# A two-layer decoder trunk on one core: in the slabs beside the top-k chain, the lo part of one expert table slab in four is subtracted on GpSimd

## The chip, the cores and the metric

The kernel runs on one core of a Trainium2 chip. A core has TensorE (PE in the profile; its weight loads are PEld), VectorE (DVE), ScalarE (ACT), GpSimd (POOL) and the queue of SyncE (SP), which issues the loads. Each works through its own instructions in order and waits for the others by semaphores. The metric is the device time of one execution in microseconds (us), lower being better. TensorE's granted clock is shown by the profile for every stretch.

## The reference

A trunk of two residual layers works on 256 tokens of width 1024. Layer 0 mixes the tokens with a gated delta rule and block-sparse attention, layer 1 with latent attention. Behind each mixer stands the same expert network (PEER), and only this one is touched by the change:

```
scores = einsum('bshpd,hpnd->bshpn', q, sub_keys)        # 8 heads, 2 halves, 128 keys
s1, i1 = top_k(scores[..., 0, :], 16);  s2, i2 = top_k(scores[..., 1, :], 16)
cand   = s1[..., :, None] + s2[..., None, :]             # 256 candidates per head
top, pos = top_k(cand, 16); expert = i1 * 128 + i2 at pos; gates = softmax(top)
act = gelu(h . u[expert]);  out = sum over experts of gates * act * v[expert]
```

There are 16384 experts, so u and v are tables of 16384 x 1024 floats per layer. 8 heads x 16 experts are chosen for each token.

## The kernel before, in words

The kernel doesn't gather the chosen rows. It multiplies all tokens with the whole table u, 128 experts at a time, and later keeps the chosen ones with a matrix of gates. 128 experts x 1024 floats are a slab; a layer has 128 of u and 128 of v.

Products run in a reduced float format (fp32r). To keep precision, a table slab is split into two parts: hi is the slab rounded to fp32r (a copy on ScalarE), and lo is the slab minus hi (a subtraction on VectorE); `split` (L130) issues both. `u_slab` (L610) loads a slab (512 KB, tile `raw`, 3 buffers), splits it (tiles `hi` and `lo`, 2 buffers each), and issues 16 matmuls with hi as the weights (L621) and then 8 with lo (L623). Each has 256 columns, one for each token. `u_pair` (L749) does two slabs and then one gelu on ScalarE (L759).

Beside the first 64 slabs of a layer stands the top-k chain (`choose`, `topk`), which chooses the experts from the scores. It runs on VectorE. For each of the two token tiles it has two parts. The first takes maxima: 16 per row, by the instructions MAX8, MATCH_REPLACE8 and FIND_INDEX8 (L486 to L499), for 8 heads and 2 halves, and then on the candidates. The second, called the selection arithmetic here, turns positions into expert numbers: comparisons, products and sums over bf16 tiles of 128 x 1024 and smaller (L566 to L583, sums at L518 and L521); all its operands lie in SBUF. Three transposes on TensorE (L604) end the work of a tile. The exponentials of the gates (L552) are ScalarE's and need its table exchanged.

The chain is a generator. `u_pair` takes steps from it after each slab until the steps' sizes pass STEP = 800. All of this is traced under `in_order("DVE")`, so VectorE executes it exactly as written: lo of a slab, a portion of the chain, lo of the next slab, a portion, and so on; after some pairs comes a modulation product (L349). On the other engines a planner puts the instructions in order with a cost model. TensorE's order, as the profile shows it, is slab after slab, 16 and 8. SP's queue issues the loads in order, each when its buffer is free, that is when hi and lo of the slab three before have read it.

Behind the 64 slabs with the chain come 64 slabs of u beside the building of the gate matrix (`g_batch`), and then the products with v, whose slabs are split in the same way. These are not touched.

The functions below are those that the change touches and what calls them.

Of the kernel before, what the change touches and what calls it, by code (L numbers as in the profile page):

```python
# [9 lines left out]
F32 = mybir.dt.float32  # L10
# [57 lines left out]
class Trunk:  # L68
# [58 lines left out]
        nc.vector.memset(self.eps, RS * EPS / 4)  # L127


    def split(self, hi, lo, src):  # L130

        return self.nc.scalar.copy(hi, src), self.nc.vector.tensor_sub(lo, src, hi.bitcast(F32))  # L132

    def mm3(self, out, l, r, start, stop):
        mm = self.nc.tensor.matmul
# [471 lines left out]
        nc.vector.tensor_scalar(dst[:, 2, s], ps[:, 2], GS, None, op0=OP.mult)  # L607
        nc.vector.scalar_tensor_tensor(dst[:, 3, s], ps[:, 2], GS, dst[:, 2, s], op0=OP.mult, op1=OP.subtract)

    def u_slab(self, st, layer, i2, hT, pair):  # L610

        nc = self.nc
        raw = self.t(st, [P, D], tag="raw", bufs=3)
        nc.sync.dma_start(raw, self.a["uT"][layer, i2])
        hi = self.t(st, [P, KD, P], F32R, tag="hi", bufs=2)
        lo = self.t(st, [P, KD, P], F32R, tag="lo", bufs=2)
        self.split(hi.rearrange("p k e -> p (k e)"), lo.rearrange("p k e -> p (k e)"), raw)
        mm = nc.tensor.matmul
        for k in range(KD):
            for s in range(2):  # L620
                mm(pair, hi[:, k], hT[:, s, k], start=k == 0 and s == 0, stop=False)  # L621
        for k in range(KD):
            mm(pair, lo[:, k], hT[:, 0, k], start=False, stop=k == KD - 1)  # L623
# [125 lines left out]
    def u_pair(self, st, layer, i2, hT, act, chain=()):  # L749

        ps = self.ps().rearrange("p (j t) -> p j t", j=2)
        for j in range(2):
            self.u_slab(st, layer, i2 + j, hT, ps[:, j])
            left = STEP
            for n in chain:
                left -= n + 64
                if left < 0:
                    break
        self.nc.scalar.activation(self.act_of(act, i2), ps, AF.Gelu)  # L759
# [1121 lines left out]
```

## Time and profile before

| | |
|---|---|
| time before, median of 3 runs | 1913.13 us (1910.81 to 1915.3) |
| profiled execution | 1913.58 us, span 1911.8 us |
| PE busy | 1878.6 us, 98% of the span |
| DVE busy | 1532.3 us, 80% |
| ACT busy | 943.5 us, 49% |
| POOL busy | 48.9 us, 3%, 131 instructions |
| mean granted clock of TensorE | 0.997 of full speed |
| shares of the chain that ended last | PE 82%, DVE 9%, DMA 4%, ACT 3% |

The profile is of one execution. Busy time is the time in which an engine has an instruction running. The chain that ended last is followed back from the last instruction, at each step to what released it. In the rows "x16" is a count of merged instructions, and what stands in brackets is how long the engine was idle before and what ended it. "out<-in" names tiles.

The slabs with the chain run from about 264 to 440 us in layer 0 and from about 1165 to 1342 us in layer 1.

### The profile page before, as it was taken

Reading aid. Unit: us, or ns where it says so; the run is one execution under the profiler, and the core shown is the slowest. Engines: PE = TensorE matmul, PEld = TensorE weight load, DVE = VectorE, ACT = ScalarE, POOL = GpSimd, SP = SyncE. Lnnn points to the kernel's source line nnn. Section 1 sums busy time; section 2 is a strip of 40 time slices with the busy share of each in tenths; the row PEclk is TensorE's granted clock in tenths of the full one; section 3 lists DMA queues with packets and bytes.
Section 4 is the critical chain, followed back from the end, with each engine's and each line's share of the span. In section 5 each row is a group of like instructions: output and inputs, shape, how many; then the busy total and the mean of one; then the engine's idle time right before and its main releaser. Section 6 shows DMA issues by size and latency. Waiting matters only on the chain.

```text
span 1911.8 us, 35995 instructions
## 1 busy us (share of the span) xinstructions
PE 1878.6 (98%) x14368; PEld 1722.2 (90%) x14368; DVE 1532.3 (80%) x3265; ACT 943.5 (49%) x1301; POOL 48.9 (3%) x131
## 2 busy tenths in 40 slices
PE   6999999999999999999999999999999999999998
PEld 6999899999999888888889899999999988888886
DVE  7879789999998789865657677999778878985565
ACT  2866555454444444454545754545444444444453
POOL 7001000000000000000000000000000000000000
PEclk9999999999999999999999999999999999999999
DMA  8456475658885555576743455565555555556673
GB/s 324 160 194 214 191 279 187 201 187 284 295 270 187 177 177 177 176 251 195 216 147 111 155 201 175 183 203 186 180 175 170 176 177 176 176 180 199 194 228 103
DMA packets 96504, 374.57 MB, mean 196 GB/s; under 512 B 11856, under 2 KB 12112, under 8 KB 89680
## 3 DMA queue, kind: packets, MB, share of 16 engines
q1 hardware_dynamic: 96336, 372.28, 58.4%
q8 instruction: 112, 1.84, 0.4%
q14 instruction: 56, 0.46, 0.1%
HBM read 371.18 MB, written 1.05 MB: 195 GB/s over the span
## 4 chain that ended last, share of the span: by engine, by line
PE 82%; DVE 9%; DMA 4%; ACT 3%; issue 1%; SPq 0%; ACTq 0%; DVEq 0%
PE ps L776 30%; PE ps L621 21%; PE ps L623 11%; PE ps L136 3%; PE ps L138 3%; PE ps L137 3%; PE ps L644 3%; DVE lo L132 3%; DMA raw<-in_v_dram 2%; PE ps L729 1%; DVE t L349 1%; PE ps L324 1%; ACT hi L132 1%; PE ps L1200 1%; DVE wlo L132 1%
## 5 line engine op out<-in xcount | busy, mean ns | idle before, releaser
L132 ACT CAST hi<-raw 128x1024 fp32r<-128x1024 f32 x508 | 534.8, 1054 | 753.1 <-PE ps L776 310.5
L132 DVE TENSOR_TENSOR lo<-raw,hi 128x1024 fp32r<-128x1024 f32 x508 | 620.0, 1222 | 249.0 <-ACT hi L132 246.8
L621 PE MATMUL ps<-hT,hi 128*128 128x256 f32 x4096 | 514.2, 278 | 0.0
L621 PEld LDWEIGHTS ps<-hT,hi 128*128 128x128 f32 x4096 | 485.8, 188 | 0.2 <-ACT hi L132 0.2
L623 PE MATMUL ps<-hT,lo 128*128 128x256 f32 x2048 | 276.7, 278 | 2.0 <-DVE lo L132 1.9
L776 PE MATMUL ps<-hi,vwh 128*128 128x512 f32 x976 | 266.1, 394 | 1.2 <-ACT hi L132 1.1
L776 PE MATMUL ps<-hi,vwl 128*128 128x512 f32 x976 | 261.3, 389 | 0.0
L776 PE MATMUL ps<-lo,vwh 128*128 128x512 f32 x976 | 260.9, 389 | 0.0
L623 PEld LDWEIGHTS ps<-hT,lo 128*128 128x128 f32 x2048 | 252.4, 188 | 4.1 <-DVE lo L132 3.7
L776 PEld LDWEIGHTS ps<-hi,vwl 128*128 128x128 f32 x976 | 183.2, 188 | 38.8
L776 PEld LDWEIGHTS ps<-lo,vwh 128*128 128x128 f32 x976 | 183.2, 188 | 38.3
L776 PEld LDWEIGHTS ps<-hi,vwh 128*128 128x128 f32 x976 | 180.3, 188 | 38.1 <-ACT hi L132 2.9
L132 DVE TENSOR_TENSOR wlo<-wraw,whi 128x1024 fp32r<-128x1024 f32 (+1 forms) x84 | 99.3, 1202 | 36.1 <-ACT whi L132 36.0
L132 ACT CAST whi<-wraw 128x1024 fp32r<-128x1024 f32 (+1 forms) x84 | 84.3, 1032 | 36.5 <-PE ps L137 14.2
L640 DVE TENSOR_TENSOR ohG<-ohB,t 128x512 f16<-128x512 f16 x256 | 99.3, 418 | 0.0
L136 PE MATMUL ps<-hT,whi 128*128 128x256 f32 x288 | 85.0, 296 | 7.1 <-ACT hT L247 7.1
L634 DVE TENSOR_TENSOR ohA<-t,t 128x1024 f16<-128x1024 f16 x128 | 87.6, 684 | 0.0
L137 PE MATMUL ps<-hT,whi 128*128 128x256 f32 x288 | 83.1, 289 | 0.2 <-DVE hT L251 0.2
L138 PE MATMUL ps<-hT,wlo 128*128 128x256 f32 x288 | 83.1, 289 | 0.0
L644 PE MATMUL ps<-ohG,ohA 128*128 128x64 f16 x2048 | 79.0, 193 | 0.3
L644 PEld LDWEIGHTS <-ohA 128*128 128x128 f16 x2048 | 67.3, 97 | 12.2 <-issue 8.7
L349 DVE SCALAR_TENSOR_TENSOR t<-t,t 128x1024 f32<-128x1024 f32 x56 | 67.4, 1217 | 2.5 <-DMA t<-in_modT_dram 2.5
(478 smaller groups left out, 2251.7 us busy)
## 6 DMA issues: line engine op xcount, KB each, us to landing
raw<-in_uT_dram SPq DMA_DIRECT2D x256, 512.0 KB, 3.3
raw<-in_v_dram SPq DMA_DIRECT2D x256, 512.0 KB, 4.1
t<-in_modT_dram SPq DMA_DIRECT2D x56, 512.0 KB, 5.0
wraw<-in_w_dram SPq DMA_DIRECT2D x13, 1024.0 KB, 6.0
raw<-in_modT_dram SPq DMA_DIRECT2D x24, 512.0 KB, 4.4
wraw<-in_wq_dram SPq DMA_DIRECT2D x12, 1024.0 KB, 5.7
mw<-in_mod_dram SPq DMA_DIRECT2D x8, 1024.0 KB, 13.6
wraw<-in_w0start_dram SPq DMA_DIRECT2D x4, 1024.0 KB, 12.0
```

Source lines behind the costliest of these rows:

```text
L132: return self.nc.scalar.copy(hi, src), self.nc.vector.tensor_sub(lo, src, hi.bitcast(F32))
L136: mm(out, l[0], r[0], start=start, stop=False)
L137: mm(out, l[0], r[1], start=False, stop=False)
L138: mm(out, l[1], r[0], start=False, stop=stop)
L324: mm(ps[g][:, i], e.hT[:, s, k, sl], w[:, b, k, :], start=s + k + b == 0, stop=s == 1 and n == KD - 1)
L349: self.nc.vector.scalar_tensor_tensor(w, w, 1.0, self.row, op0=OP.mult, op1=OP.mult, accum_out=self.modc[layer][:, c:c + 1])
L621: mm(pair, hi[:, k], hT[:, s, k], start=k == 0 and s == 0, stop=False)
L623: mm(pair, lo[:, k], hT[:, 0, k], start=False, stop=k == KD - 1)
L634: nc.vector.tensor_tensor(A, self.iota_t[:, None].to_broadcast(full), pairs(0, full), op=OP.is_equal)
L640: nc.vector.tensor_tensor(B[:, j], b0, pairs(2 + j, part), op=OP.mult)
L644: nc.tensor.matmul(ps[:, t], A[:, t // 2, :, t % 2], B[:, j, t // 2, :, t % 2], start=j == 0, stop=j == 1)
L776: self.nc.tensor.matmul(acc[i][c], w[a][:, j, i * P:(i + 1) * P], v[b][:, c * 512:(c + 1) * 512], start=first and j + a + b == 0, stop=False)
```

## The change

`split` gets an argument for the engine of the subtraction, with VectorE as the default; `u_slab` hands it on; `u_pair` sets it to GpSimd for the second slab of a pair where there is a chain and i2 % 4 is not 0. i2 runs over 0, 2, 4, ..., 62, so these are the slabs 3, 7, 11, ..., 63 of each layer: 16 of 64, and 32 in all. The order of what stays on VectorE is the same.

```diff
-    def split(self, hi, lo, src):
+    def split(self, hi, lo, src, engine=None):
 
-        return self.nc.scalar.copy(hi, src), self.nc.vector.tensor_sub(lo, src, hi.bitcast(F32))
+        return self.nc.scalar.copy(hi, src), (engine or self.nc.vector).tensor_sub(lo, src, hi.bitcast(F32))
...
-    def u_slab(self, st, layer, i2, hT, pair):
+    def u_slab(self, st, layer, i2, hT, pair, engine=None):
...
-        self.split(hi.rearrange("p k e -> p (k e)"), lo.rearrange("p k e -> p (k e)"), raw)
+        self.split(hi.rearrange("p k e -> p (k e)"), lo.rearrange("p k e -> p (k e)"), raw, engine)
...
-            self.u_slab(st, layer, i2 + j, hT, ps[:, j])
+            self.u_slab(st, layer, i2 + j, hT, ps[:, j], self.nc.gpsimd if chain and j and i2 % 4 else None)
```

## Rows read from the trace of the kernel before

**Rows 1.** Busy time by stretch: us; busy PE, PEld, DVE, ACT, POOL; clock.

```profile
1195.00:1205.00 10.00, 10.00 (x90) 10.00 (x90) 9.59 (x38) 4.78 (x6) 0.00 (x0) 1.00 0.64 211
1228.00:1248.00 20.00, 20.00 (x172) 20.00 (x172) 18.51 (x34) 8.99 (x11) 0.00 (x0) 1.00 0.62 199
```

**Rows 2.** Chain of waits, first and later slabs of both layers: start, us, what.

```profile
264.12 1.83 PE ps L621 x16
...
323.48 1.12 PE ps L623 x8
...
429.73 1.83 PE ps L621 x16
...
1165.50 1.83 PE ps L621 x16
...
1222.64 1.81 PE ps L621 x16
1224.46 0.91 PE ps L623 x8
...
1227.18 1.05 PE ps L623 x8
1228.22 1.88 PE ps L621 x16
...
1331.17 1.83 PE ps L621 x16
```

**Rows 3.** Instructions by time, layer 1, slabs 21 to 24: start, us, engine, line.

```profile
1224.49 1.05 ACT L132 CAST hi<-raw 128x1024 fp32r<-128x1024 f32 x1 [1.67 <-PE ps L621]
...
1225.14 0.68 DVE L579 TENSOR_TENSOR tge<-tb,t 128x1024 bf16<-128x1024 bf16 x1
...
1225.74 1.22 DVE L132 TENSOR_TENSOR lo<-raw,hi 128x1024 fp32r<-128x1024 f32 x1
1226.88 1.22 DVE L583 TENSOR_TENSOR tm<-tge,tixb 128x1024 bf16<-128x1024 bf16 x1
...
1227.01 1.21 PE L623 MATMUL ps<-hT,lo 128*128 128x256 f32 x8
...
1230.93 1.22 DVE L132 TENSOR_TENSOR lo<-raw,hi 128x1024 fp32r<-128x1024 f32 x1
```

**Rows 4.** Instructions by time, where POOL ran beside VectorE.

```profile
83.07 1.28 POOL L1169 TENSOR_TENSOR t<-t,t 128x512 f32<-128x512 f32 x1 [35.15 <-issue]
...
83.16 1.13 DVE L1177 SCALAR_TENSOR_TENSOR F<-ps,t,k 128x128 f32<-128x128 f32 x4
...
168.59 0.74 POOL L1357 TENSOR_TENSOR t<-t,t 128x256 f32<-128x256 f32 x1 [79.63 <-ACT t L1356]
...
169.59 1.22 DVE L132 TENSOR_TENSOR wlo<-wraw,whi 128x1024 fp32r<-128x1024 f32 x1
...
170.48 1.46 POOL L1287 TENSOR_TENSOR t<-qkv,t 128x512 f32<-128x512 f32 x1 [1.15 <-ACT qkv L1116]
170.73 2.29 DVE L349 SCALAR_TENSOR_TENSOR raw<-raw,t 128x1024 f32<-128x1024 f32 x1
```

**Rows 5.** The page's DMA issues: loads of slabs of u.

```profile
raw<-in_uT_dram SPq DMA_DIRECT2D x256, 512.0 KB, 3.3
```

**Rows 6.** Instructions by time, layer 1, slabs 50 to 57.

```profile
1300.93 2.01 ACT L132 CAST hi<-raw 128x1024 fp32r<-128x1024 f32 x2
...
1302.01 1.23 DVE L132 TENSOR_TENSOR lo<-raw,hi 128x1024 fp32r<-128x1024 f32 x1 [1.91 <-ACT hi L132]
...
1308.57 1.22 DVE L132 TENSOR_TENSOR lo<-raw,hi 128x1024 fp32r<-128x1024 f32 x1
...
1309.85 1.21 PE L623 MATMUL ps<-hT,lo 128*128 128x256 f32 x8
...
1322.07 1.22 DVE L132 TENSOR_TENSOR lo<-raw,hi 128x1024 fp32r<-128x1024 f32 x1
...
1324.08 1.11 PE L623 MATMUL ps<-hT,lo 128*128 128x256 f32 x8
```

## The prediction

> **What bounds the kernel now.** I read three views in turn: busy time by stretch, the chain of waits, and the instructions in order of time where DVE and PE come close.
>
> The stretches come first [rows 1]. In both of them TensorE is busy for every microsecond at the full granted clock (1.00), while VectorE is nearly full too (9.59 of 10 us among the maxima, 18.51 of 20 us in the selection arithmetic). POOL does nothing. So two engines are near their limit, and the question is which of them ends last.
>
> The chain of waits answers it [rows 2]: inside the 64 slabs that run beside the top-k chain it is TensorE alone. A slab is 16 matmuls on hi (1.81 us) and 8 on lo (0.91 us), 2.72 us together. From slab 0 to slab 60 the ideal in layer 1 is 60 x 2.72 = 163.2, plus two sets of transposes at some 0.33 each (an estimate: 3 matmuls at 0.11), 163.9 us; the rows give 1331.17 - 1165.50 = 165.67. In layer 0 they give 429.73 - 264.12 = 165.61. So all that VectorE's load costs TensorE now is about 1.8 us per layer, 3.5 us in all, **and that is the most the change can win here**. Its form is visible: a lo group that waited (1.05 instead of 0.91, in layer 0 one of 1.12), and behind it slabs at a slower pace (1.88 instead of 1.81) until the next break.
>
> How late may a lo be? There are two hi buffers, so hi of slab n starts when the hi matmuls of slab n-2 end and is done 2 x 2.72 - 1.81 - 1.05 = 2.58 us before slab n; its lo is wanted 1.81 us after slab n starts. So lo has about 4.4 us from the end of hi; VectorE needs 1.22 of them, if it comes at once.
>
> **The change.** Slabs 3, 7, ... 63 of each layer (the second of a pair, i2 = 2, 6, ...), 16 per layer and 32 in all, get their lo from POOL. Everything else keeps its order on VectorE, whose order is written out.
>
> *Removed:* 32 subtractions on VectorE, which free 1.14 us each (1225.74 to the next start at 1226.88 is the distance of two starts [rows 3]): 36 us of VectorE. Nearly all of it lies beside TensorE and is worth nothing by itself.
>
> *Added:* 32 subtractions on POOL. Its rows with two inputs are 0.74 us for 256 columns and 1.28 us for 512 [rows 4], so 1024 columns cost 1.28 + 2 x 0.54 = 2.36 us, an estimate; the slower 1.46 us row would make it 2.9, and I take 2.36 since that operation began inside a VectorE subtraction (169.59 to 170.81). No row has POOL writing fp32r; VectorE's fp32r subtraction takes what its f32 operations of that size take. Alone, 2.36 fits well into 4.4 us. Behind it in POOL's queue nothing is waiting. The raw buffer is freed 1.1 us later than by a VectorE that comes at once; three buffers cycle in 8.16 us, and 3.3 us for the load [rows 5], 1.05 for hi and 2.36 for lo make 6.7, so SP's queue of loads has 1.4 us to spare, and only one turn in four of a buffer is longer.
>
> *The new wait.* The rows show POOL and VectorE keeping each other out [rows 4]. While POOL ran a 512-column operation (170.48 to 171.94), VectorE's two-input operation begun at 170.73 took 2.29 instead of 1.22: it did its work only after 171.8. POOL in its turn took 1.46 instead of 1.28, as it had to wait for VectorE's subtraction. But at 83.16 four VectorE operations, with one of their two full operands in PSUM, ran 1.13 us inside POOL's 1.28 and were not held. So an operation with two operands in SBUF waits until about 0.13 us before POOL's end: up to 2.2 us.
>
> [...]
>
> Among the maxima (one input), about 10 of the 16 POOL slabs per layer, I therefore take nothing: POOL starts when hi ends, is done 2.36 later, and VectorE's next lo is ready 2.72 later. (The modulation products that stand there in layer 0 have two SBUF inputs and can be held; the lo behind each has 4.4 - 1.2 = 3.2 us to spare, which covers a hold of 2.2.) In the selection arithmetic (two parts per layer, about 10 slabs each), every VectorE operation has two SBUF inputs, so each POOL slab takes 2.2 from VectorE and gives 1.14 back: 1.06 us lost, where VectorE already sets the pace. There I go slab by slab.
>
> *Second part, both layers* [rows 6]. hi of slabs 50 and 51 comes as a pair that ends at 1302.94; lo of slab 50 runs until 1303.2 (1302.01 + 1.23). Then POOL takes slab 51, VectorE's arithmetic behind it waits 2.2, saves 1.14, and lo of slab 52 ends at 1308.57 + 1.22 + 1.06 = 1310.85; TensorE asked for it at 1309.85 and already waited. So TensorE loses 1.0. The next POOL slab (55) takes 1.06 more; lo of slab 57 ended at 1323.29 and is used at 1324.08, 0.8 spare, so 0.2 more is lost. Layer 0 has the same order: 2 x 1.2 = **+2.4**.
>
> *First part, layer 1* [rows 3]. hi of slab 23 ends at 1225.54, when VectorE is in a two-input operation (1225.14 to about 1225.8); lo of slab 22 is next at 1225.74 and TensorE waits for it at 1227.01. If POOL goes first, lo of slab 22 ends 2.2 later: 2.2 lost. If VectorE goes first, lo of slab 24 comes 1.06 later, at 1230.93 + 1.22 + 1.06 = 1233.2, against 1227.1 + 2 x 2.82 = 1232.8 for its use at the slower pace: 0.4 lost. Nothing decides between them; I take about the middle, **+1.2**.
>
> *First part, layer 0.* The same slabs, so +1.2; but VectorE arrives late there now, and its freed time takes away that lateness: two waits of 0.2 (1.12 for 0.91 in [rows 2], and a second alike) and some slow pace, -0.6. Together **+0.6**.
>
> Sum: 2.4 + 1.2 + 0.6 = +4.2 us. Bounds of the sum: 2 x 1.0 + 0.4 + 0.4 - 0.6 = +2.2 with the cheap order everywhere, and 2.4 + 2.2 + 2.2 = +6.8 with the dear one and nothing won. The profiled execution took 1913.58 us (span 1911.8 and 1.8 around it), so the changed one would take 1917.8; that execution lies 0.45 above the median of the three runs, 1913.13, so against the median I predict 1917.3.
>
> **Rivals.**
>
> *A, the waits vanish.* POOL's operations fall into gaps, or the selection has more slack than I counted; VectorE is relieved, and TensorE runs 2.72 throughout. For it: 36 us less on a nearly full engine. Against it: TensorE's row is already full [rows 1]. Time: between 1913.1 - 3.5 = 1909.6 and about 1915, that is mostly no change. Only if other stretches gain with it, because the instruction order that the planner makes on the other engines shifts, does it pass the bound of what can be told.
>
> *B, the maxima wait too.* Then 32 POOL slabs cost 1.06 each, 34 us of VectorE; the half before each selection (some 5 POOL slabs, 5 us) has a slack of about 3 us, so some 2 us more are lost in each of four halves: 4.2 + 8 = +12, 1925. Against it: the four operations at 83.16 [rows 4]. It decides once lo comes more than 4.4 us after hi.
>
> *C, the slow pace spreads.* A short wait is followed by slabs of 1.88 + 0.94 = 2.82 instead of 2.72 until a break [rows 2]. If POOL's lo causes one such wait early in each half, up to 100 more slabs run 0.10 slower: up to +10 beside my 4.2. Time 1920 to 1927.
>
> *D, the change does nothing visible,* +-1 us: it would need POOL to read without taking VectorE's time. Against it: the held operation at 170.73 [rows 4]. It lies in the band of A.
>
> **Chances.** Forecast (+2 to +7) 0.50; A and D 0.35; B 0.08; C 0.07. A measurement of this kernel can tell 0.2%, 3.8 us. The forecast lies on that edge: of its 0.50 I put 0.34 beyond it and 0.16 within; B and C are beyond; of A and D 0.12 is faster by more than 3.8, 0.22 within and 0.01 slower. That makes faster 0.12, same 0.38, slower 0.50. The range reaches from 1910.5, near A's end, to 1923.5, short of B; the forecast's own range is 1915.1 to 1920.
>
> **What would show it.** POOL: 32 subtractions of about 2.4 us. In the selection, VectorE operations beside POOL stretched by up to 2.2 us (the row of two-input bf16 operations shows a longer maximum), and lo groups of TensorE that wait about 1 us at slabs 52 of both layers. Among the maxima: VectorE idle before lo, waiting for hi, and no stretched maxima; stretched ones would mean B. From slab 0 to slab 60, about 167 to 168 us per layer instead of 165.6; 164 us means A. If these stretches stay at 165.6 and the total moves, the order elsewhere has changed, and my account is wrong.

## The result, and the profile after

The changed kernel took 1924.84 us (median of 4 runs, 1923.46 to 1925.32), the kernel before 1912.26 us beside it (4 runs, 1910.81 to 1915.3): ratio 1.0063, 95% interval 1.0045 to 1.0080. It is slower. The forecast had the direction, 1917.3 us, but the result lies outside its range of 1910.5 to 1923.5. A later series of the same kernel on another chip gave 1921.13 us against 1913.65, ratio 1.0039 [1.0028, 1.0050], so the medians give a loss of 7 to 13 us where 4 were forecast.

The page of the profile after (profiled execution 1924.38 us) has these lines; the third is the new group on POOL (line, engine, operation, tiles, count | busy, mean ns | idle before), the last the loads of slabs of u, 3.3 us before [rows 5].

```profile
span 1922.6 us, 35989 instructions
PE 1884.8 (98%) x14368; PEld 1726.6 (90%) x14368; DVE 1535.1 (80%) x3233; ACT 943.8 (49%) x1301; POOL 133.0 (7%) x163
...
L132 POOL TENSOR_TENSOR lo<-raw,hi 128x1024 fp32r<-128x1024 f32 x32 | 82.9, 2591 | 367.9 <-ACT hi L132 367.9
...
raw<-in_uT_dram SPq DMA_DIRECT2D x256, 512.0 KB, 3.5
```

VectorE has 32 subtractions fewer and is busy for 1535.1 us, before 1532.3: the 32 x 1.14 = 36 us that they free came back as instructions that last longer. Beside POOL's subtractions 21 VectorE operations took over 0.1 us longer than the same operations before, 38.5 us together. On TensorE and ScalarE the two traces have the same instructions in the same order, so no stretch was rearranged.

Where the 10.8 us of span (of the profiled executions) went is seen by cutting TensorE's time at the start of slab 0 and at the transposes that end each selection (from the instructions in order of time). An undisturbed half is 30 slabs of 2.72 and 0.33, 81.9 us.

| us | before | after | difference |
|---|---|---|---|
| before slab 0 of layer 0 | 263.88 | 264.29 | +0.41 |
| layer 0, first part | 82.52 | 85.93 | +3.41 |
| layer 0, second part | 82.84 | 84.63 | +1.79 |
| layer 1, first part | 82.59 | 86.30 | +3.71 |
| layer 1, second part | 82.83 | 84.40 | +1.57 |
| between the layers' chains | 736.02 | 735.67 | -0.35 |
| behind the last transposes | 581.12 | 581.38 | +0.26 |

The four parts hold 10.5 of it. The first part of layer 1, instructions in order of time (start, us, engine, line), the slabs of [rows 3]:

```profile
1220.00 2.61 POOL L132 TENSOR_TENSOR lo<-raw,hi 128x1024 fp32r<-128x1024 f32 x1 [8.47 <-ACT hi L132]
1220.39 2.77 DVE L569 TENSOR_TENSOR tm<-tge,t 128x1024 bf16<-128x1024 bf16 x1
...
1230.88 2.43 POOL L132 TENSOR_TENSOR lo<-raw,hi 128x1024 fp32r<-128x1024 f32 x1 [8.27 <-ACT hi L132]
1230.99 3.40 DVE L132 TENSOR_TENSOR lo<-raw,hi 128x1024 fp32r<-128x1024 f32 x1
...
1234.45 1.29 PE L623 MATMUL ps<-hT,lo 128*128 128x256 f32 x8 [2.01 <-DVE lo L132]
```

At slab 23 POOL came 0.11 us before VectorE's lo of slab 22. VectorE's subtraction took 3.40 instead of 1.22 us and ended 0.98 us behind POOL's end (1233.31, 1234.39); TensorE waited 2.01 us for it. The hold at 1220.39 cost nothing: its lo waits for hi anyway, behind ScalarE's exchange of tables. The chain of waits tells it from TensorE's side, and shows a second cost (start, us, what):

```profile
1231.08 3.32 DVE lo L132
...
1234.45 1.29 PE ps L623 x8
1235.74 3.33 PE ps L621 x16
1239.08 0.94 PE ps L623 x8
1240.02 1.88 PE ps L621 x16
```

The hi group behind the wait takes 3.33 us instead of 1.88. Busy time by stretch gives the reason; its last three columns are the granted clock, the DMA share and GB/s. The first two lines are the stretches of [rows 1].

```profile
1195.00:1205.00 10.00, 10.00 (x91) 10.00 (x90) 8.41 (x36) 4.59 (x6) 2.41 (x1) 1.00 0.61 195
1228.00:1248.00 20.00, 17.99 (x142) 17.79 (x141) 18.75 (x30) 7.22 (x10) 4.54 (x2) 0.91 0.48 163
...
1235.00:1236.00 1.00, 1.00 (x9) 1.00 (x8) 0.95 (x2) 0.52 (x1) 0.00 (x0) 0.71 0.58 111
1236.00:1237.00 1.00, 1.00 (x6) 1.00 (x6) 0.91 (x4) 0.00 (x0) 0.00 (x0) 0.50 0.98 389
1237.00:1238.00 1.00, 1.00 (x7) 1.00 (x6) 1.00 (x2) 0.00 (x0) 0.00 (x0) 0.50 1.06 414
...
1321.00:1325.00 4.00, 4.00 (x37) 4.00 (x36) 3.90 (x8) 1.68 (x3) 0.41 (x1) 1.00 0.82 262
```

Among the maxima VectorE is relieved (8.41 of 10 us, before 9.59) and TensorE keeps its 10.00. In the selection TensorE loses 2.0 of 20 us, and from 1235.4 to 1238.8 us the clock is at half, the lower of its two levels, 1.2 GHz (the stretch that it begins in shows 0.71). 2.01 of wait and 3.33 - 1.88 = 1.45 of half clock are 3.46 of the 3.71 us of this part.

The second part of layer 1, where [rows 6] stood for before:

```profile
1312.01 2.49 POOL L132 TENSOR_TENSOR lo<-raw,hi 128x1024 fp32r<-128x1024 f32 x1 [7.93 <-ACT hi L132]
1312.16 3.22 DVE L518 TENSOR_TENSOR tm<-tm 128x512 bf16<-128x512 bf16 x3
...
1318.79 1.22 DVE L132 TENSOR_TENSOR lo<-raw,hi 128x1024 fp32r<-128x1024 f32 x1
...
1320.06 1.21 PE L623 MATMUL ps<-hT,lo 128*128 128x256 f32 x8 [1.08 <-DVE lo L132]
...
1321.11 2.05 PE L621 MATMUL ps<-hT,hi 128*128 128x256 f32 x16
```

This is the step as predicted: VectorE's arithmetic is held behind slab 51 (a run of three sums, 3.22 instead of 1.00 us), and at slab 52 TensorE waits 1.08. Here the clock stays at 1.00 (the line 1321.00:1325.00 above); only the slow pace follows (2.05 as it is shown here, 1.98 at the full pace). In the first part of layer 0 the same meeting at slab 23 went the other way:

```profile
326.63 1.22 DVE L132 TENSOR_TENSOR lo<-raw,hi 128x1024 fp32r<-128x1024 f32 x1
326.94 3.16 POOL L132 TENSOR_TENSOR lo<-raw,hi 128x1024 fp32r<-128x1024 f32 x1 [8.23 <-ACT hi L132]
327.76 3.42 DVE L583 TENSOR_TENSOR tm<-tge,tixb 128x1024 bf16<-128x1024 bf16 x1
```

VectorE's lo was 0.31 us ahead; POOL waited for it, then held the product at 327.76. No lo group of TensorE was late by more than 0.2 to 0.3 us there. But this part runs at the slow pace from its first slabs on, before POOL's first subtraction at 270.42 us. The first two lines are of the kernel before, the others of the changed kernel, as TensorE's timeline shows them:

```profile
263.88 2.08 PE L621 MATMUL ps<-hT,hi 128*128 128x256 f32 x16
...
266.70 1.98 PE L621 MATMUL ps<-hT,hi 128*128 128x256 f32 x16
...
264.29 2.13 PE L621 MATMUL ps<-hT,hi 128*128 128x256 f32 x16
266.26 1.10 PE L623 MATMUL ps<-hT,lo 128*128 128x256 f32 x8
267.20 2.05 PE L621 MATMUL ps<-hT,hi 128*128 128x256 f32 x16
```

A slab is 2.83 us then (267.20 to 270.03 for the next); some 24 slabs at 0.105 more are 2.5 of this part's 3.4 us.

### The profile page after: what moved, and what is told of

It is laid out like the page before. It is cut to its first block, busy times and chain, and to the rows that moved or that the text cites. A ratio compares the mean times of both kernels' runs of the same rounds, so it can differ in the third digit from the quotient of the medians.

```text
span 1922.6 us, 35989 instructions
## 1 busy us (share of the span) xinstructions
PE 1884.8 (98%) x14368; PEld 1726.6 (90%) x14368; DVE 1535.1 (80%) x3233; ACT 943.8 (49%) x1301; POOL 133.0 (7%) x163
## 4 chain that ended last, share of the span: by engine, by line
PE 80%; DVE 12%; ACT 3%; DMA 3%; issue 2%; SPq 0%; ACTq 0%; DVEq 0%
PE ps L776 33%; PE ps L621 19%; PE ps L623 10%; DVE lo L132 3%; PE ps L136 3%; PE ps L644 3%; PE ps L138 3%; PE ps L137 3%; PE ps L729 1%; DVE t L349 1%; PE ps L324 1%; DMA raw<-in_v_dram 1%; DVE tm L518 1%; PE ps L1200 1%; DVE wlo L132 1%
## 5 line engine op out<-in xcount | busy, mean ns | idle before, releaser
L132 DVE TENSOR_TENSOR lo<-raw,hi 128x1024 fp32r<-128x1024 f32 x476 | 583.0, 1226 | 261.3 <-ACT hi L132 257.2
L132 POOL TENSOR_TENSOR lo<-raw,hi 128x1024 fp32r<-128x1024 f32 x32 | 82.9, 2591 | 367.9 <-ACT hi L132 367.9
```

What stands on the lines that cost most here:

```text
L132: return self.nc.scalar.copy(hi, src), (engine or self.nc.vector).tensor_sub(lo, src, hi.bitcast(F32))
```

## The experiments

Theory T, as it stood when the experiments began: POOL excludes VectorE's operations with two inputs in SBUF, those alone, for its whole instruction; a loss arises only where one held operation makes one lo late, and its size is the wait there and what the clock does behind it. Rivals: the maxima pay too (B); lo by POOL simply comes later, 2.4 instead of 1.2 us after hi (R); each POOL slab of the selection costs VectorE the same, wherever it stands. Kernels of one series share the runs of the kernel before.

**POOL beside the maxima alone (e1), beside the selection alone (e2).**

```diff
-self.nc.gpsimd if chain and j and i2 % 4 else None
+self.nc.gpsimd if chain and i2 + j in (3, 7, 11, 15, 31, 35, 39, 43, 47) else None    # e1
+self.nc.gpsimd if chain and i2 + j in (19, 23, 27, 51, 55, 59, 63) else None          # e2
```

> POOL keeps only the 9 slabs of a layer that stand beside the maxima (3, 7, 11, 15, 31, 35, 39, 43, 47), the 7 beside the selection arithmetic go back to VectorE. Theory T (POOL and a VectorE operation with two operands in SBUF exclude one another, so only the selection pays): 1909 to 1914 us, the time before within 0.2%, no stretched VectorE operation. Rival R (lo simply comes later from POOL, 2.4 instead of 1.2 us, and each of the 32 slabs pays its share of 12.6 us, 0.39): 18 x 0.39 = +7, 1919 us. Rival B of the prediction (maxima wait too): 1917 to 1921.

> The complement: POOL only in slabs 19, 23, 27, 51, 55, 59, 63 of each layer, beside the selection arithmetic. T: nearly the whole loss, 1920 to 1926 us, with the same waits of TensorE for lo (about 1 us in the second parts, 2 us in the first part of layer 1 with 1.4 us of half clock behind it); in layer 0 VectorE arrives late at the selection, as before the change, so its first part may lose 1 to 3 us more. R: 14 x 0.39 = +5.5, 1918 us.

e1: 1913.69 us, ratio 0.9998 [0.9989, 1.0007]. e2: 1923.36, ratio 1.0044 [1.0028, 1.0059]. The loss is the selection's. In e1 all 18 subtractions on POOL took the same time (min/median/max ns, first and last start):

```profile
L132 POOL TENSOR_TENSOR lo<-raw,hi x18: 2402/2407/2409, 270.6 to 1292.4; 128x1024 fp32r<-128x1024 f32 x18
its engine sat idle before it (us, times) until:
  ACT hi L132: 308.1, 18
```

So the estimate of 2.36 was right, and POOL itself is never held here. B and R fall: no MAX8, MATCH_REPLACE8 or FIND_INDEX8 takes longer beside POOL, and lo comes 2.4 us after hi in these slabs too, without a cost that can be told.

But "no stretched VectorE operation" was not right. Six are stretched in e1: four modulation products of layer 0, which have two inputs (up to 2.25 instead of 1.22 us), and in each layer a cast of indices, which has one. The first line is of the kernel before, the others of e1:

```profile
1283.01 0.29 DVE L532 CAST tixb<-tix 128x256 bf16<-128x256 uint32 x1
...
1281.48 2.41 POOL L132 TENSOR_TENSOR lo<-raw,hi 128x1024 fp32r<-128x1024 f32 x1 [8.47 <-ACT hi L132]
1281.94 2.10 DVE L532 CAST tixb<-tix 128x256 bf16<-128x256 uint32 x1
```

The changed kernel holds the same two casts, for 2.10 us each. So "two inputs, those alone" is too narrow. TensorE waits for none of the six: the lo behind them had the time to spare.

In e2 the first part of layer 0 loses 5.3 us. Slab 23 meets the dear order there too, and ahead of it a second way to a loss shows: POOL's subtraction for slab 19 holds the small operation whose result ScalarE's exponentials need (1.76 instead of 0.27 us), so ScalarE's next hi is late, and TensorE waits 1.43 us for it:

```profile
315.85 1.76 DVE L551 TENSOR_TENSOR te<-ttop 128x128 f32<-128x128 f32 x1
...
320.85 2.15 PE L621 MATMUL ps<-hT,hi 128*128 128x256 f32 x16 [1.43 <-ACT hi L132]
...
327.08 2.63 POOL L132 TENSOR_TENSOR lo<-raw,hi 128x1024 fp32r<-128x1024 f32 x1 [9.62 <-PE ps L623]
327.40 3.40 DVE L132 TENSOR_TENSOR lo<-raw,hi 128x1024 fp32r<-128x1024 f32 x1
...
330.85 1.50 PE L623 MATMUL ps<-hT,lo 128*128 128x256 f32 x8 [2.09 <-DVE lo L132]
332.15 3.33 PE L621 MATMUL ps<-hT,hi 128*128 128x256 f32 x16
```

In layer 1 the wait at slab 22 came as expected, the half clock behind it did not: the hi group runs at the full pace, with the granted clock at 1.00.

```profile
1237.19 1.20 PE L623 MATMUL ps<-hT,lo 128*128 128x256 f32 x8 [2.01 <-DVE lo L132]
1238.23 1.98 PE L621 MATMUL ps<-hT,hi 128*128 128x256 f32 x16
```

So the same wait can cost 1.45 us more or nothing more.

**The same number of slabs, two further on (e3).**

```diff
-self.nc.gpsimd if chain and j and i2 % 4 else None
+self.nc.gpsimd if chain and j and i2 % 4 == 0 else None
```

> The same number of POOL slabs, moved by two: slabs 1, 5, 9, ..., 61. Nothing else differs. T: what a POOL slab costs depends on how much room the lo behind it has, so the dear case (POOL just ahead of a lo for which TensorE already waits) falls on other slabs: 53 in the second parts has the place of 23, and 21 in the first parts that of 51. I expect 1917 to 1927 us with the losses distributed otherwise: second parts above first parts. R: no change against the changed kernel, 1924 to 1925, in the same places.

1923.51 us, ratio 1.0053 [1.0037, 1.0068]. The loss changed its place: the first parts take 84.15 and 84.00 us, the second 85.91 and 85.87. Now a slab of the second parts has the dear order, with its wait and half clock:

```profile
405.31 2.43 POOL L132 TENSOR_TENSOR lo<-raw,hi 128x1024 fp32r<-128x1024 f32 x1 [8.28 <-ACT hi L132]
405.43 3.40 DVE L132 TENSOR_TENSOR lo<-raw,hi 128x1024 fp32r<-128x1024 f32 x1
...
408.88 1.20 PE L623 MATMUL ps<-hT,lo 128*128 128x256 f32 x8 [2.02 <-DVE lo L132]
...
409.92 3.30 PE L621 MATMUL ps<-hT,hi 128*128 128x256 f32 x16
```

**Four of the 32 back on VectorE (e9):** slabs 23 and 51 of both layers, where the late lo were.

```diff
-self.nc.gpsimd if chain and j and i2 % 4 else None
+self.nc.gpsimd if chain and i2 + j in (3, 7, 11, 15, 19, 27, 31, 35, 39, 43, 47, 55, 59, 63) else None
```

> The changed kernel, with slabs 23 and 51 of each layer back on VectorE (28 POOL slabs are left, 10 of them in the selection arithmetic). Theory T (a loss arises where one held VectorE operation makes one lo late, and its place sets its size): slab 23 of layer 1 made lo of slab 22 wait behind POOL (2.0 us, and 1.45 us of half clock behind it), slab 51 made the 1.1 us wait at slab 52; without them the first part of layer 1 takes about 82.9 us from slab 0 to the first transposes instead of 86.3, the second part of layer 1 about 83.3 instead of 84.4, that of layer 0 about 83.4 instead of 84.6, and the time is 1917 to 1920 us against 1924.8. Rival (each POOL slab of the selection costs VectorE 1.06 us, wherever it stands): 10 of 14 slabs are left, so 10/14 of the 10.8 us, 1921.6 us, and slab 27 or 19 becomes the late one, with each part at some 5/7 of its loss (first part of layer 1 85.0).

1915.88 us, ratio 1.0011 [1.0000, 1.0021]. The parts take 82.83, 83.77, 83.37 and 83.23 us. Layer 0's second part and both parts of layer 1 had gained 7.1 us by the change, and 5.0 of these are gone, with 28 subtractions still on POOL, 10 of them in the selection arithmetic. Layer 0's first part falls by 3.1 us, but this profile doesn't have the slow pace from slab 0, so most of that (some 2.5 us) isn't the four slabs' doing. The time is lower than either theory had it; the rival of equal costs (1921.6) falls. At the place of the 2.01 us wait:

```profile
1226.41 1.22 DVE L132 TENSOR_TENSOR lo<-raw,hi 128x1024 fp32r<-128x1024 f32 x1
1227.55 1.22 DVE L583 TENSOR_TENSOR tm<-tge,tixb 128x1024 bf16<-128x1024 bf16 x1
...
1227.69 1.19 PE L623 MATMUL ps<-hT,lo 128*128 128x256 f32 x8
```

**POOL writes but hardly reads (e5).** POOL subtracts the first 32 columns alone; the other 992 columns of lo are set to zero by three memsets, so the lo of these 32 slabs is left out but for 32 columns. POOL stays busy about as long.

```diff
+        engine.tensor_sub(lo[:, :32], src[:, :32], hi[:, :32].bitcast(F32))
+        for _ in range(3):
+            engine.memset(lo[:, 32:].bitcast(F32), 0.0)
```

> In the 32 POOL slabs POOL subtracts only the first 32 columns of lo and then fills the other 992 three times with zeros, so lo of these slabs is left out but for 32 columns; POOL is busy, after hi, about as long, and reads almost nothing. T (the exclusion is of the reads of two-input VectorE operations against POOL's reads): VectorE is not stretched, 1908 to 1914 us. R (POOL's length is what counts): 1920 to 1926 us.

1909.26 us, ratio 0.9974 [0.9963, 0.9985]. The second parts are at 81.95, the undisturbed half. Beside the memsets the product of layer 0 that was held for 3.42 us takes 1.27 (this kernel's L588 is L583 of the others):

```profile
325.27 0.74 POOL L135 TENSOR_TENSOR lo<-raw,hi 128x32 fp32r<-128x32 f32 x1
325.82 1.27 DVE L588 TENSOR_TENSOR tm<-tge,tixb 128x1024 bf16<-128x1024 bf16 x1
325.96 1.91 POOL L137 MEMSET lo<- 128x992 f32 x2
```

So neither POOL's being busy nor its writing holds VectorE; what is left is its reading. The time is 5.0 us below the kernel before (2.9 to 7.1 by the interval), which the 3.5 us that the prediction gave as the most lies within. In the profile the four parts are 1.7 us shorter than before; where the rest comes from isn't shown.

**A third hi buffer, with the change (e4_hi3) and without it (e4_hi3_before).** hi of the next slab can start earlier, so a late lo has more room.

```diff
-        hi = self.t(st, [P, KD, P], F32R, tag="hi", bufs=2)
+        hi = self.t(st, [P, KD, P], F32R, tag="hi", bufs=3)
```

(and in the four other places that use this tag)

> The changed kernel with a third buffer for hi everywhere, so that hi, and with it POOL's start, can come one slab (2.72 us) sooner and lo has 7 us instead of 4.4. T: a late VectorE is what TensorE waits for, and a held operation of 2.2 us fits into the new room: the waits shrink to below half and the half clock goes, 1912 to 1919 us. Rival (room doesn't help, since the load of the table slab or VectorE's total work is the limit): 1921 to 1926.

> Control: the kernel before with the same third buffer for hi. It shows what the buffer does without POOL. T: TensorE hardly waits there, 1908 to 1914 us.

1916.0 us, ratio 1.0016 [1.0007, 1.0025], and 1909.65 us, ratio 0.9982 [0.9972, 0.9991]. The longest wait for a lo falls from 2.0 to 0.6 us with the change. Without it the parts of TensorE but for layer 0's first are at 81.70 to 81.96; that one runs at the slow pace from slab 0.

**Third buffer, and POOL beside the maxima alone (e10):** the edits of e4_hi3 and e1 together.

> Three hi buffers, and POOL in the slabs 3, 7, 11, 15, 31, 35, 39, 43, 47 alone (18 in both layers), beside one-input maxima. Theory T: POOL costs nothing there, and the freed 1.14 us per slab let VectorE reach the selection arithmetic earlier than with three hi buffers alone (1909.65 us), which took away all waits but those of layer 0's first part: 1907 to 1910 us, the four parts at 82 to 82.6 us each. Rival (the gain of the third buffer and the relief are the same slack, counted once): 1909.5 to 1910.5, nothing beyond the third buffer. Against both: 1912 or more would mean that POOL's lo comes too late for the ScalarE copy that now runs a slab further ahead.

1910.34 us, ratio 0.9986 [0.9976, 0.9996]; the four parts at 81.71, 81.96, 81.70 and 81.96. The time lies in the rival's range and just outside T's: the third buffer alone takes away the same waits, and POOL adds nothing that can be told. Both kernels with three buffers and no POOL in the selection lie some 0.15% below the kernel before, under the 0.2% that the prediction took as what can be told; that TensorE's waits are gone is seen in the parts.

**Larger portions of the chain beside the maxima, smaller ones in the selection (e6 with POOL, e7 without).** The steps are 1300 and 500 instead of 800 in e6, with POOL in the slabs with 1300; 860 and 680 in e7.

```diff
-self.nc.gpsimd if chain and j and i2 % 4 else None
-            left = STEP
+self.nc.gpsimd if chain and j and self.step == 1300 else None    # e6; none on GpSimd in e7
+            left = self.step      # 1300 in the maxima, 500 in the selection (e7: 860, 680)
```

> A version that should beat both: POOL takes the second slab of each pair only beside the maxima, never in the selection arithmetic, and VectorE takes larger steps of the chain beside the maxima (STEP 1300) and smaller ones in the selection (500), so that the selection is spread over some 16 slabs instead of 10. Theory T: no lo comes late, all slabs take 2.72, the halves take 82 us: 1907 to 1912 us, 2 to 6 below the kernel before. Against it: if TensorE's pace is what it is anyway, the time before, 1912 to 1915.

> The control of the last: no POOL at all, steps 860 and 680, which moves the same kind of work a little, as far as VectorE alone can carry it. T: VectorE is nearly full beside the maxima already, so its lateness only moves from the selection to the maxima: 1911 to 1915 us, no difference that can be told from before. If it reaches the time of the spread version with POOL, POOL isn't needed for it.

e6 missed: 1924.32 us, ratio 1.0064 [1.0049, 1.0078]. 1300 is too much beside one lo in two slabs, even without a lo of its own in the other: VectorE has no gap left in the maxima (busy for 21.93 of the 22 us from 360 us on), lo comes late there (longest wait 2.33 us), and POOL holds what stands between the maxima (a cast of indices took 2.50 us, an addition 2.39). At the start of the two selections of layer 1 ScalarE's exponentials come late, and TensorE waits 1.91 and 2.01 us for hi. e7: 1912.48, ratio 0.9996 [0.9988, 1.0005], no difference that can be measured.

**The changed kernel again (e8, e11).** No edit.

> The changed kernel once more, for a second profile. If the slow pace from slab 0 of layer 0 (1.89 and 0.94 instead of 1.81 and 0.91) is a matter of the execution, this profile may start at 1.81, and the first part of layer 0 then takes about 83.5 us instead of 85.9; if the changed kernel brings it about, it is there again at 264 us. The waits at slabs 22 and 52 of layer 1 (2.0 and 1.1 us) and the half clock behind the first should return as they were.

> The changed kernel a third time. The slow pace from slab 0 of layer 0 stood in both profiles of it so far, and in three profiles of other kernels, one of them without any subtraction on POOL; seven others had none. If it is a matter of the execution, this profile starts at 1.81 us per hi group with a chance of about 7 in 12, and the first part of layer 0 then takes some 83.5 us; a third slow start would speak for the kernel (5/12 to the third, 0.07, by chance). The time in either case 1921 to 1925 us.

1922.31 us in the one run of e8; 1921.13 (8 runs, 1919.96 to 1924.47), ratio 1.0039 [1.0028, 1.0050] in e11. The parts in the profiles are 85.88, 84.89, 85.63, 84.41 and 85.90, 84.40, 86.30, 84.40, the wait at slab 22 of layer 1 being 2.03 and 2.01 us, with half clock behind it, and the slow pace in layer 0 was there each time. In both, TensorE also waited for a lo of POOL's own, at slab 27 of layer 0 (0.37 and 0.83 us). In all, 7 of 14 profiles show it from the first slabs of layer 0: the three of the changed kernel, e4_hi3, e6, and two kernels without any subtraction on POOL (e4_hi3_before, e7; the expectation of e11 left out e7). In no profile does layer 1 begin with it. So it needs no POOL; whether the change makes it likelier stays open. e11's profiled execution is the longest of its eight (1924.47, the next 1922.9), while e7's, which has the slow pace too, is the shortest of its eleven; how often the timed runs have it is open.

## Why the prediction was wrong

*Right.* That TensorE's 16 and 8 set the time, and that nothing can be won beyond a few us (e5, e10). POOL's 2.36 us: 2.40 to 2.41. That the maxima pay nothing that can be told (e1) and the selection the loss (e2). The second parts: forecast 1.0 and 0.2 of wait; measured 1.08 at slab 52, and 0.2 at slab 56.

*Right in its result, too wide in its reason: "one input".* From operations with one operand in PSUM the prediction concluded that one-input operations aren't held. The MAX8, MATCH_REPLACE8 and FIND_INDEX8 aren't, but the casts of indices are (2.10 instead of 0.29 us), and so are the two-input modulation products among the maxima. In e1 TensorE waits for none of them. The Trainium skill (SBUF — State Buffer, section "Who interferes with whom") says that a VectorE instruction with two SBUF inputs contends with a GpSimd instruction that reads SBUF and not with one that only writes it, and that one with at most one SBUF input doesn't contend outside the modes that use both of VectorE's ports, which copies and casts can enter. The runs agree: 3.40 us for the held subtraction, 1.27 for the product beside memsets (e5), no MAX8 over 0.30 us beside POOL; the held cast fits the last part, but no run here shows in which mode it ran.

*Too small: the second parts.* +1.79 and +1.57 where +1.2 each was summed. The slow pace behind the wait was left out: about 5 slabs at 0.1.

*The step that failed: the first part of layer 1.* The prediction had the two orders, 2.2 with POOL first and 0.4 with VectorE first, and wrote: "Nothing decides between them; I take about the middle, +1.2". Two things were wrong. The middle of two orders isn't one that happens: POOL was ahead by 0.11 us and the wait was 2.01, the dear order nearly to the number. And the dear order had a price beyond the wait: behind 2.0 us without a matmul the granted clock fell to half, and the next hi group took 3.33 for 1.88, +1.45. That was in no term and in neither bound, so the bound of +6.8 was too low by it. The two make 3.46 us here, and e9, which undoes this meeting, takes the part back to 83.37. The wait came at the same place in all three profiles of the changed kernel, with half clock behind it each time; it came in e2 too, but there the clock stayed at 1.00: the 1.45 us are a price that can come, not one that always does, and what decides it isn't shown. (The Trainium skill's section says as well that the order of issue decides who is held: slab 23 of layer 0, with VectorE 0.31 us ahead, and of layer 1, with POOL 0.11 us ahead, show both outcomes.)

*The first part of layer 0.* Forecast +0.6, measured +3.4. The order there was the cheap one, and its waits are within the forecast. 2.5 us are the slow pace from the first slabs. Rival C had this size and put it down to POOL's lo; it began before POOL's first subtraction, and stands in two kernels without one, so C's cause falls, and the cause of the slow start stays open. The gain of 0.6 from an earlier VectorE can't be seen under it.

*The sum.* 3.4 for the second parts, 3.7 and 3.4 for the first make 10.5, against 2.4 + 1.2 + 0.6 = 4.2. Of the 6.3 us between them, 2.5 belong to layer 1's first part, 2.8 to layer 0's, 1.0 to the second parts. The range left out the case in which the dear order, the half clock behind it and a slow pace came together. That the time measured is the 1925 of rival B is chance: B's cause, maxima that wait, isn't there (e1).

## What to carry to other kernels

Work moved to GpSimd was free here beside the maxima (18 subtractions of 1024 columns: ratio 0.9998) and dear beside the selection's two-input operations, and a few meetings carried the cost: taking 4 of 32 subtractions back undid 5.0 of 7.1 us in three of the four parts. The count of inputs alone doesn't tell what is held, as the casts show. So ask of each moved instruction what VectorE runs during it and which consumer is next late, ScalarE's operations among them (e2's 1.43 us), and price both orders to the end rather than their middle. On a TensorE that hardly pauses, price a stall with what can follow: behind 2.0 us the next group lost 1.45 more or nothing, behind 1.08 nothing to the clock. And where the trouble is a late operand, another buffer took the waits away (ratio 0.9982, a gain at the edge of what can be told), which moving work to a third engine did not.

## What the runs showed of the hardware that was not expected

- The granted clock: of eleven waits of TensorE of 1.78 to 2.33 us beside the chain, in the changed kernel, e2, e3, e6, e8 and e11, seven were followed by some 3 us at half clock and a hi group of 3.21 to 3.54 us in the timeline instead of 1.98 to 2.05. Behind the other four (2.01 in e2; 1.91, 2.01 and 2.33 in e6) it stayed at 1.00, and so it did behind all waits up to 1.43 us. The length of the wait alone doesn't decide it.
- A held subtraction takes nearly its own full time after POOL ends: 3.40 us for one begun 0.11 us after a POOL of 2.43.
- The slow pace, 2.83 instead of 2.72 us a slab at a granted clock of 1.00, can begin without a wait for lo ahead of it, at slab 0 of layer 0, and last 24 slabs (e4_hi3_before: all 30 of the part).
- A cast with one input in SBUF (128 x 256, integers to bf16) is held by a reading POOL: 2.10 instead of 0.29 us.
